# Inverse roots of the norms: a power on GpSimd in place of logarithm, exponential and a Newton step

## The chip, the cores and the metric

The kernel runs on one core of a Trainium2 chip. The metric is the device time of one execution in microseconds (us), lower is better. A core has TensorE (PE, matrix products), VectorE (DVE), ScalarE (ACT), GpSimd (POOL) and SyncE (SP, which only issues transfers here). Each engine runs its own instructions strictly in the order in which they were written; semaphores make it wait for the others.

## The reference, cut to what matters

One step of a one-layer decoder: an RMS norm of x, one wide projection, two attention mixers, gates, and two more projections. Two kinds of norm matter here, that of x over 1024 columns, and that of every q and k head over 64:

```python
def rms_norm(x, gain):
    xf = x.astype(jnp.float32)
    y = xf * lax.rsqrt(jnp.mean(xf * xf, axis=-1, keepdims=True) + NORM_EPS)
    return (y * gain.astype(jnp.float32)).astype(x.dtype)

h = rms_norm(x, norm_gain)
parts = jnp.split(jnp.einsum("ntd,de->nte", h, w_in), SPLIT_POINTS, axis=-1)
a_qkv = [(rms_norm(heads(parts[3 * g]), qk_norm_a[g, 0]),
          rms_norm(heads(parts[3 * g + 1]), qk_norm_a[g, 1]),
          heads(parts[3 * g + 2])) for g in range(A_GROUPS)]
```

There are 1024 prompt positions and 8 decode rows, 1032 columns in all. Everything is float32.

## The kernel before

Activations are held transposed: features on the 128 partitions, the 1032 positions as columns, cut into three chunks (slots) of 344 columns. Float32 products are made of three passes, with each operand split into a rounded part (`hi`, made by an ACT copy) and a rest (`lo`, made by a subtraction on VectorE or POOL).

The projections run over 82 weight tiles of 128 output columns in the order of `ORDER`. Four gate tiles come first, in the start stage, while x is normed. Then follow the tiles of mixer B (g = 3: k, v, q and gates between), then four groups c = 0 to 3 of mixer A, each with q, k and v tiles for g = 0, 1, 2 and two or three gate tiles (`ga`, `gb`), then `zb`, `za`, `br` and `out`. A tile has three slots, a slot 24 dense matmuls (line 248), and a slot three parts of eight matmuls. At each part's end, `part_end` emits attention work and whatever was put there by `after(n, f)`: f is called n parts later. So nothing is planned by costs; the order is what this walk writes.

Per tile the next tile's weights are converted in two halves (`w_conv`, lines 126 and 127: ACT rounds, POOL subtracts), at one and three parts after the tile's first part, and the loading of the tile after that is issued from SP at five parts (there is one staging buffer, which POOL's subtraction releases).

For a q or k chunk, `ev_qk` squares the matmul's result on ACT (line 885), multiplies it with the head's gain on VectorE (line 886) and splits the squares into `sqh` and `sql` (lines 889, 890). Three parts later `ssq` sums the squares over the heads' 64 rows by two matmuls into PSUM (894, 895) and starts the root: Ln, Exp and Square on ACT (225 to 227), and POOL multiplies the gained result by the approximate root (900). Two parts after that `norm` makes Newton's step on VectorE in two operations (230 and 904), the second of which multiplies into the result. There are 87 such chunks: 15 of g = 3 and 72 of mixer A. After the last chunk of a tile, `after_qk` starts the split pieces `prep_q` (ACT 319, POOL 320) and `prep_k` or `prep_k2` (ACT and VectorE, lines 355, 356, 337, 338), which feed the attention's matmuls.

For x itself `h_root` does the same three times in the start stage, once per chunk of columns, with the Newton step written to the root (235); `h_scale` then applies the root (VectorE 215, ACT 216, and POOL or VectorE 221). The roots' tiles are `rn` (two buffers) and `root`; `rt` and `sq` hold the root's square.

Of the kernel before, what the change touches and what calls it, by code (L numbers as in the profile page):

```python
# [10 lines left out]
F32 = mybir.dt.float32  # L11
# [3 lines left out]
ALU = mybir.AluOpType  # L15
# [4 lines left out]
D = 1024  # L20
# [47 lines left out]
def hybrid_step(ctx: ExitStack, tc: tile.TileContext, a):  # L68
# [21 lines left out]
    eps = cst.tile([128, 1], F32, name="eps")  # L90
# [7 lines left out]
    nc.vector.memset(eps, EPS)  # L98
# [86 lines left out]
    def sv(j, k):  # L185
        return sq[min(j, 1)][k]
# [10 lines left out]
    def h_add(j, k):  # L197
        if k > 1:
            nc.vector.tensor_tensor(sv(j, k % 2), sv(j, k % 2), sv(j, k), op=ALU.add)
        if k == KK - 1:  # L200
            nc.vector.tensor_tensor(sv(j, 0), sv(j, 0), sv(j, 1), op=ALU.add)

    def h_root(j):
        pm = psum("w", 4)
        nc.tensor.matmul(pm[:, :CH], ones, sv(j, 0), start=True, stop=True)  # L205
        t = tmp("sq", [128, CH])
        rsqrt_act(roots[j], t, pm[:, :CH], D)
        rsqrt_dve(roots[j], t, pm[:, :CH], D)
# [14 lines left out]
    def rsqrt_act(r, t, ssq, n):  # L223

        nc.scalar.activation(r, ssq, AF.Ln, scale=1.0 / n, bias=eps)  # L225
        nc.scalar.activation(r, r, AF.Exp, scale=-0.5)  # L226
        nc.scalar.activation(t, r, AF.Square)  # L227

    def newton(t, ssq, n):
        nc.vector.scalar_tensor_tensor(ssq, ssq, n * EPS, t, op0=ALU.add, op1=ALU.mult)  # L230

    def rsqrt_dve(r, t, ssq, n):

        newton(t, ssq, n)
        nc.vector.scalar_tensor_tensor(r, ssq, -3.0 * n, r, op0=ALU.add, op1=ALU.mult)
# [642 lines left out]
    def ev_qk(kind, g, c, ch, pt):  # L878
# [11 lines left out]
        after(0, lambda: nc.vector.tensor_tensor(sl, s, sh.bitcast(F32), op=ALU.subtract))  # L890

        def ssq():
# [4 lines left out]
            t = tmp("rt", [128, CH])  # L897
            rsqrt_act(r, t, pm[:, :CH], 64)

            nc.gpsimd.tensor_tensor(dst[:, col], dst[:, col], r, op=ALU.mult)  # L900

            def norm():
                newton(t, pm[:, :CH], 64)
                nc.vector.scalar_tensor_tensor(dst[:, col], pm[:, :CH], -3.0 * 64, dst[:, col], op0=ALU.add, op1=ALU.mult)
                if ch == NCH - 1:
                    after(1, lambda: after_qk(kind, g, c))
# [272 lines left out]
    def conv_consts():  # L1179
        nc.vector.tensor_copy(blk, blk_f)  # L1180
        nc.vector.tensor_scalar(hsel, blk_f[:, ::64], 0.125, None, op0=ALU.mult)
        nc.vector.tensor_scalar(qkg, qkg, -1.0 / 128, None, op0=ALU.mult)
# [55 lines left out]
    nc.vector.tensor_scalar(gain, gain, -0.5 / D, None, op0=ALU.mult)  # L1238
# [181 lines left out]
```

## Time and profile before

| what | value |
|---|---|
| time, median of 2 runs | 1251.02 us (1248.45 to 1253.59) |
| time of the profiled execution | 1251.58 us |
| its span, first to last instruction | 1249.8 us |
| mean granted clock of TensorE | 0.988 of full speed |
| TensorE busy | 1184.3 us, 95% |
| VectorE busy | 786.5 us, 63% |
| ScalarE busy | 785.3 us, 63% |
| GpSimd busy | 631.7 us, 51% |

A row of the profile names the engine, the line of the kernel, the operation, what it writes and reads (out<-in), its shape, how often it ran, its time, and what ended the engine's idle time before it. The time differs from the span by the 1.8 us around the first and last instruction.

### The profile page before, as it was taken

The page shows a single profiled execution, that of the slowest core. Times are in us where ns is not written, and L with a number is a line of the kernel's source. Part 1 is how long each engine was busy: PE and PEld are TensorE (multiplying, and loading weights), DVE is VectorE, ACT ScalarE, POOL GpSimd, SP SyncE. Part 2 cuts the span into 40 slices and gives each one's busy share as a digit, 9 for nine tenths or more (in the row PEclk, how much of TensorE's full clock was granted, in tenths as well). Part 3 has the DMA queues.
Part 4 walks back from the last instruction along what each step waited for, and adds up shares of the span by engine and source line. Part 5 has one row for each costly group of instructions (what it writes and reads, how often), then busy time and mean ns, then how long its engine had stood idle before and what let it go on. Part 6 is the DMA issues. An engine that isn't in the chain of part 4 may idle for free.

```text
span 1249.8 us, 21998 instructions
## 1 busy us (share of the span) xinstructions
PE 1184.3 (95%) x7649; PEld 1150.3 (92%) x7649; DVE 786.5 (63%) x1881; ACT 785.3 (63%) x1879; POOL 631.7 (51%) x613
## 2 busy tenths in 40 slices
PE   7899999999989998989999899998999999999998
PEld 6799999999989997979999798888898898999998
DVE  6853555777757767886779876888756573343111
ACT  5555676787958794868777697857796533443110
POOL 3555244443624564855476673658453585444220
PEclk9999999999999998999999999999899999999999
DMA  6146446366483756556765639464658646543343
GB/s 224 41 144 198 170 152 228 134 207 187 139 249 140 230 171 193 174 168 191 217 190 197 209 137 275 132 216 163 198 153 230 195 158 216 186 144 110 109 147 102
DMA packets 117648, 219.44 MB, mean 176 GB/s; under 512 B 27337, under 2 KB 96801, under 8 KB 116129
## 3 DMA queue, kind: packets, MB, share of 16 engines
q1 hardware_dynamic: 117536, 218.03, 54.5%
q8 instruction: 61, 1.00, 0.3%
q14 instruction: 51, 0.41, 0.1%
HBM read 180.14 MB, written 113.25 MB: 235 GB/s over the span
## 4 chain that ended last, share of the span: by engine, by line
PE 57%; DVE 15%; ACT 13%; DMA 5%; POOL 5%; issue 4%; SPq 1%; POOLq 0%; DVEq 0%; ACTq 0%
PE ps_d L248 43%; PE ps_w L248 4%; ACT P L449 2%; DMA w_st<-in_w 2%; PE ps_w L483 2%; DVE k_b L356 2%; PE ps_o L556 1%; ACT q_st L319 1%; DMA dkv<-in_ca 1%; DVE sql L890 1%; POOL q_st L320 1%; DVE dpr L854 1%; PE ps_w L430 1%; PE ps_w L431 1%; DVE P L439 1%
## 5 line engine op out<-in xcount | busy, mean ns | idle before, releaser
L248 PE MATMUL ps_d<-h_hi,w 128*128 128x344 f32 x3456 | 862.9, 326 | 9.9 <-ACT h_hi L191 6.0
L248 PEld LDWEIGHTS ps_d<-h_hi,w 128*128 128x128 f32 x3456 | 605.7, 191 | 14.8 <-ACT h_hi L191 7.0
L248 PE MATMUL ps_d<-h_lo,w 128*128 128x344 f32 x1728 | 569.8, 330 | 5.9 <-POOL h_lo L221 3.3
L248 PEld LDWEIGHTS ps_d<-h_lo,w 128*128 128x128 f32 x1728 | 329.7, 191 | 10.3 <-POOL h_lo L221 5.8
L127 POOL TENSOR_TENSOR w<-w_st,w 128x512 fp32r<-128x512 f32 (+1 forms) x159 | 212.2, 1337 | 183.7 <-ACT w L126 164.7
L449 ACT ACTIVATE P<-P,st 128x256 f32<-128x256 f32 (+1 forms) x256 | 115.6, 453 | 67.0 <-DVE st L439 51.9
L126 ACT ACTIVATE w<-w_st 128x512 fp32r<-128x512 f32 (+1 forms) x160 | 100.5, 632 | 84.2 <-DMA w_st<-in_w 82.8
L900 POOL TENSOR_TENSOR qn<-qn,rn 128x344 f32<-128x344 f32 x48 | 45.9, 957 | 162.7 <-ACT rn L226 132.4
L320 POOL TENSOR_TENSOR q_st<-qn,q_st 64x512 fp32r<-64x512 f32 x64 | 92.1, 1442 | 24.7 <-ACT q_st L319 18.6
L510 DVE TENSOR_TENSOR pt<-ps_w,pt 128x384 fp32r<-128x384 f32 (+1 forms) x112 | 49.3, 440 | 50.5 <-ACT pt L509 50.0
L509 ACT ACTIVATE pt<-ps_w 128x384 fp32r<-128x384 f32 (+1 forms) x112 | 43.9, 392 | 48.5 <-DVE pt L510 44.1
L483 PE MATMUL ps_w<-ident,P 128*128 128x128 f32 x400 | 63.6, 275 | 3.8 <-DVE sls L770 1.1
L1116 DVE TENSOR_TENSOR xres<-ps_d,xres 128x344 f32<-128x344 f32 x24 | 12.4, 517 | 76.1 <-PE ps_d L248 45.3
L900 POOL TENSOR_TENSOR kn<-kn,rn 128x344 f32<-128x344 f32 x39 | 37.3, 957 | 42.8 <-ACT rn L226 36.3
L890 DVE TENSOR_TENSOR sql<-sq,sqh 128x344 fp32r<-128x344 f32 x87 | 57.9, 666 | 0.6
L483 PEld LDWEIGHTS ps_w<-ident,P 128*128 128x128 f32 x400 | 49.9, 140 | 9.0 <-ACT P L449 2.9
L885 ACT ACTIVATE sq<-ps_d 128x344 f32<-128x344 f32 x87 | 39.3, 452 | 28.7 <-PE ps_d L248 23.3
L319 ACT ACTIVATE q_st<-qn 64x512 fp32r<-64x512 f32 x64 | 54.0, 867 | 0.7
L230 DVE SCALAR_TENSOR_TENSOR ps_w<-ps_w,rt 128x344 f32<-128x344 f32 x87 | 44.9, 516 | 14.7 <-ACT rt L227 14.3
L556 PE MATMUL ps_o<-pt,v 128*128 128x256 f32 (+1 forms) x288 | 46.7, 281 | 6.9 <-DVE pt L510 6.3
L431 PE MATMUL ps_w<-k_b,q_st 128*128 128x128 f32 (+1 forms) x192 | 51.9, 281 | 0.0
L225 ACT ACTIVATE rn<-ps_w,eps 128x344 f32<-128x344 f32 x89 | 47.8, 537 | 6.1 <-PE ps_w L205 4.7
(225 smaller groups left out, 2167.6 us busy)
## 6 DMA issues: line engine op xcount, KB each, us to landing
w_st<-in_w SPq DMA_DIRECT2D x81, 512.0 KB
out_sa<-in_ca SPq DMA_DIRECT2D x16, 1020.0 KB
dkv<-in_ca SPq DMA_DIRECT2D x24, 512.0 KB
sc<-sc_dr SPq DMA_DIRECT2D x32, 192.0 KB
k_b<-k_a SPq DMA_DIRECT2D x18, 256.0 KB
k_a<-k_b SPq DMA_DIRECT2D x18, 256.0 KB
x<-in_xT SPq DMA_DIRECT2D x24, 172.0 KB
oz<-o_dr SPq DMA_DIRECT2D x8, 516.0 KB
```

Of the source, the lines that this page charges most:

```text
L126: nc.scalar.activation(wh, s, AF.Copy)
L127: eng.tensor_tensor(wl, s, wh.bitcast(F32), op=ALU.subtract)
L248: nc.tensor.matmul(pt[:, :CH], ops[i][0], ops[i][1], start=(i == 0), stop=(i == N - 1))
L319: nc.scalar.activation(j.view_o(t[s, :T])[:, c], v, AF.Copy)
L320: nc.gpsimd.tensor_tensor(j.view_o(t[r, :T])[:, c], v, j.view_o(t[s, :T])[:, c].bitcast(F32), op=ALU.subtract)
L431: nc.tensor.matmul(pt[:, o:o + 128 * nk], j.sq[h][:, q], j.sk[h][:, k], start=False, stop=True)
L449: nc.scalar.activation(u.p[:, c], u.p[:, c], AF.Exp, scale=-1.0, bias=st[:, qb, h:h + 1], accum_out=st[:, qb, 2 + h:3 + h])
L483: nc.tensor.transpose(pt[:, o:o + 128], u.p[:, o:o + 128], ident)
L510: nc.vector.tensor_tensor(t[:, 512 + p0:512 + p0 + m], pt[:, o:o + m], t[:, p0:p0 + m].bitcast(F32), op=ALU.subtract)
L556: nc.tensor.matmul(pt[:, c], j.vv[kb // 4][:, v0:v0 + 128], t[:, 512 * n + p0:512 * n + p0 + 128 * nq], start=(first and n == 0), stop=Tru ...
L890: after(0, lambda: nc.vector.tensor_tensor(sl, s, sh.bitcast(F32), op=ALU.subtract))
L900: nc.gpsimd.tensor_tensor(dst[:, col], dst[:, col], r, op=ALU.mult)
```

## The change

The inverse root is no longer made by Ln, Exp, Square and a Newton step. ACT copies the sums out of PSUM, and POOL raises the copy to the power -0.5, with the exponent in a one-column tile `mhalf`, read as if it were 344 columns wide. eps is added where the squares are last touched: in the last addition of `h_add` (as D / 128 * EPS, since 128 rows are summed there) and in the subtraction that makes `sql`. The mean's divisor and Newton's -0.5 go into the gains as constants (32 and 8, the square roots of 1024 and 64). The product with the root moves from `ssq` to `norm`, two parts later, and is made by VectorE for g = 3 and by POOL for the rest. The root's square needs no tile any more.

```diff
         if k == KK - 1:
-            nc.vector.tensor_tensor(sv(j, 0), sv(j, 0), sv(j, 1), op=ALU.add)
+            nc.vector.scalar_tensor_tensor(sv(j, 0), sv(j, 0), D / 128 * EPS, sv(j, 1), op0=ALU.add, op1=ALU.add)
...
         nc.tensor.matmul(pm[:, :CH], ones, sv(j, 0), start=True, stop=True)
-        t = tmp("sq", [128, CH])
-        rsqrt_act(roots[j], t, pm[:, :CH], D)
-        rsqrt_dve(roots[j], t, pm[:, :CH], D)
+        rsqrt(roots[j], pm[:, :CH])
...
-    def rsqrt_act(r, t, ssq, n):
-
-        nc.scalar.activation(r, ssq, AF.Ln, scale=1.0 / n, bias=eps)
-        nc.scalar.activation(r, r, AF.Exp, scale=-0.5)
-        nc.scalar.activation(t, r, AF.Square)
-
-    def newton(t, ssq, n):
-        nc.vector.scalar_tensor_tensor(ssq, ssq, n * EPS, t, op0=ALU.add, op1=ALU.mult)
-
-    def rsqrt_dve(r, t, ssq, n):
-
-        newton(t, ssq, n)
-        nc.vector.scalar_tensor_tensor(r, ssq, -3.0 * n, r, op0=ALU.add, op1=ALU.mult)
+    def rsqrt(r, ssq):
+
+        nc.scalar.activation(r, ssq, AF.Copy)
+        nc.gpsimd.tensor_tensor(r, r, mhalf.to_broadcast([128, CH]), op=ALU.pow)
...
-        after(0, lambda: nc.vector.tensor_tensor(sl, s, sh.bitcast(F32), op=ALU.subtract))
+        after(0, lambda: nc.vector.scalar_tensor_tensor(sl, s, EPS, sh.bitcast(F32), op0=ALU.add, op1=ALU.subtract))
...
             r = tmp("rn", [128, CH], bufs=2)
-            t = tmp("rt", [128, CH])
-            rsqrt_act(r, t, pm[:, :CH], 64)
-
-            nc.gpsimd.tensor_tensor(dst[:, col], dst[:, col], r, op=ALU.mult)
+            rsqrt(r, pm[:, :CH])
 
             def norm():
-                newton(t, pm[:, :CH], 64)
-                nc.vector.scalar_tensor_tensor(dst[:, col], pm[:, :CH], -3.0 * 64, dst[:, col], op0=ALU.add, op1=ALU.mult)
+                (nc.vector if g == 3 else nc.gpsimd).tensor_tensor(dst[:, col], dst[:, col], r, op=ALU.mult)
                 if ch == NCH - 1:
                     after(1, lambda: after_qk(kind, g, c))
...
-        nc.vector.tensor_scalar(qkg, qkg, -1.0 / 128, None, op0=ALU.mult)
+        nc.vector.tensor_scalar(qkg, qkg, 8.0, None, op0=ALU.mult)
...
-    nc.vector.tensor_scalar(gain, gain, -0.5 / D, None, op0=ALU.mult)
+    nc.vector.tensor_scalar(gain, gain, 32.0, None, op0=ALU.mult)
```

The order on POOL in the second group of mixer A (c = 1), from the weights' subtractions ahead of the q tile of g = 1 to the first piece of its split; first before:

```order
L127 TENSOR_TENSOR w<-w_st,w 128x512 x2
L900 TENSOR_TENSOR qn<-qn,rn 128x344 x2
L127 TENSOR_TENSOR w<-w_st,w 128x512
L900 TENSOR_TENSOR qn<-qn,rn 128x344
L127 TENSOR_TENSOR w<-w_st,w 128x512
L900 TENSOR_TENSOR kn<-kn,rn 128x344
L956 COPY dc<-qn 128x8
L320 TENSOR_TENSOR q_st<-qn,q_st 64x512
```

and the same place on POOL with the change, where line 224 is the power and line 889 the product:

```order
L127 TENSOR_TENSOR w<-w_st,w 128x512 x2
L224 TENSOR_TENSOR rn<-rn,mhalf 128x344
L889 TENSOR_TENSOR qn<-qn,rn 128x344
L224 TENSOR_TENSOR rn<-rn,mhalf 128x344
L889 TENSOR_TENSOR qn<-qn,rn 128x344
L127 TENSOR_TENSOR w<-w_st,w 128x512
L224 TENSOR_TENSOR rn<-rn,mhalf 128x344
L127 TENSOR_TENSOR w<-w_st,w 128x512
L889 TENSOR_TENSOR qn<-qn,rn 128x344
L224 TENSOR_TENSOR rn<-rn,mhalf 128x344
L941 COPY dc<-qn 128x8
L309 TENSOR_TENSOR q_st<-qn,q_st 64x512
```

Each chunk has a power of its own on POOL, ahead of the weights' subtractions and of the pieces of the split; the product now stands behind the power, and the one of k's first chunk has moved behind the first piece.

The order on ACT at the same place before, for the first chunk of that q tile:

```order
L885 ACTIVATE sq<-ps_d 128x344
L889 ACTIVATE sqh<-sq 128x344
L225 ACTIVATE rn<-ps_w,eps 128x344
L226 ACTIVATE rn<-rn 128x344
L227 ACTIVATE rt<-rn 128x344
L449 ACTIVATE P,st<-P,st 128x128
```

and on ACT with the change, where line 223 is the copy out of PSUM:

```order
L874 ACTIVATE sq<-ps_d 128x344
L878 ACTIVATE sqh<-sq 128x344
L223 ACTIVATE rn<-ps_w 128x344
L438 ACTIVATE P,st<-P,st 128x128
L438 ACTIVATE P,st<-P,st 128x256
```

Three instructions have become one, and the attention's exponentials (449, now 438) stand directly behind it.

The order on POOL in the start stage with the change, from the weights' last subtraction to the second chunk's first rests (h_lo), where before no row of the root stood on POOL:

```order
L224 TENSOR_TENSOR rn<-rn,mhalf 128x344
L219 TENSOR_TENSOR h_lo<-x_117,h_hi 128x344
L219 TENSOR_TENSOR h_lo<-x_119,h_hi 128x344
L219 TENSOR_TENSOR h_lo<-x_120,h_hi 128x344
L219 TENSOR_TENSOR h_lo<-x_121,h_hi 128x344
L219 TENSOR_TENSOR h_lo<-x_123,h_hi 128x344
L219 TENSOR_TENSOR h_lo<-x_124,h_hi 128x344
L224 TENSOR_TENSOR root<-root,mhalf 128x344
L224 TENSOR_TENSOR rn<-rn,mhalf 128x344
L219 TENSOR_TENSOR h_lo<-x_117,h_hi 128x344
```

The power of the first chunk of columns (`root`) stands directly ahead of that of the third (`rn`), and h_lo behind both.

## Rows read from the trace of the kernel before

**Rows 1.** The page's first part: busy us, share of the span, instructions.

```profile
PE 1184.3 (95%) x7649; PEld 1150.3 (92%) x7649; DVE 786.5 (63%) x1881; ACT 785.3 (63%) x1879; POOL 631.7 (51%) x613
```

**Rows 2.** Two stretches: us, busy us (instructions) of each engine, PEclk, DMA share, GB/s.

```profile
69.00:245.00 176.00, 176.00 (x1187) 173.52 (x1186) 92.74 (x267) 113.81 (x290) 73.84 (x69) 1.00 0.51 174
...
245.00:962.00 717.00, 673.59 (x4420) 651.01 (x4419) 532.79 (x1346) 547.01 (x1353) 397.68 (x398) 0.98 0.60 189
```

**Rows 3.** TensorE's waits, 245 to 962 us: total us, times, longest.

```profile
PE ps_w L791 <- DVE dmx L788: 7.8, 2, 5.1
PE ps_w L895 <- DVE sql L890: 6.4, 5, 2.7
PE ps_o L556 <- DVE pt L510: 6.3, 10, 2.1
```

**Rows 4.** Stretches: the twelve q and k pairs; first, last, sum.

```profile
245.30:278.80 33.50, 33.50 (x235) 33.17 (x234) 24.95 (x67) 27.34 (x71) 16.58 (x15) 1.00 0.63 210
...
869.00:909.40 40.40, 36.78 (x228) 35.01 (x227) 30.46 (x69) 28.73 (x70) 19.98 (x20) 0.92 0.67 233
sum 417.40, PE 394.00 PEld 379.23 DVE 329.89 ACT 310.62 POOL 199.10; mean PE 32.83 PEld 31.60 DVE 27.49 ACT 25.89 POOL 16.59
```

**Rows 5.** Stretches between the pairs: one v tile, two with gate tiles, sum.

```profile
510.60:527.50 16.90, 16.65 (x116) 16.27 (x115) 15.00 (x33) 14.19 (x31) 16.36 (x15) 1.00 0.18 51
...
736.00:771.10 35.10, 32.97 (x213) 31.89 (x212) 22.36 (x61) 28.81 (x74) 20.45 (x23) 0.95 0.55 139
...
909.40:962.30 52.90, 48.08 (x319) 46.89 (x319) 30.45 (x105) 40.24 (x112) 22.39 (x27) 0.97 0.64 177
sum 299.60, PE 279.59 PEld 271.78 DVE 202.86 ACT 236.54 POOL 198.27; mean PE 23.30 PEld 22.65 DVE 16.90 ACT 19.71 POOL 16.52
```

**Rows 6.** Groups by line on POOL: times run, busy us, mean ns, idle before.

```profile
L127 POOL TENSOR_TENSOR w<-w_st,w 128x512 fp32r<-128x512 f32 x155 | 202.4, 1309 | 177.4 <-ACT w L126 158.3 <-DVE sql L890 9.8 <-PE ps_o L556 3.0
...
L900 POOL TENSOR_TENSOR qn<-qn,rn 128x344 f32<-128x344 f32 x48 | 45.9, 957 | 162.7 <-ACT rn L226 132.4
```

**Rows 7.** The same by line on ACT.

```profile
L225 ACT ACTIVATE rn<-ps_w,eps 128x344 f32<-128x344 f32 x89 | 47.8, 537 | 6.1 <-PE ps_w L205 4.7
L226 ACT ACTIVATE rn<-rn 128x344 f32<-128x344 f32 x89 | 43.8, 492 | 2.8
L227 ACT ACTIVATE rt<-rn 128x344 f32<-128x344 f32 x87 | 42.8, 492 | 2.7
...
L1078 ACT ACTIVATE rt<-ps_d 128x344 f32<-128x344 f32 x14 | 6.4, 456 | 5.1 <-PE ps_d L248 3.8 <-issue 1.1
```

**Rows 8.** The same by line on DVE.

```profile
L230 DVE SCALAR_TENSOR_TENSOR ps_w<-ps_w,rt 128x344 f32<-128x344 f32 x87 | 44.9, 516 | 14.7 <-ACT rt L227 14.3
...
L904 DVE SCALAR_TENSOR_TENSOR qn<-ps_w,qn 128x344 f32<-128x344 f32 x48 | 24.8, 517 | 5.7 <-DVE ps_w L230 0.9
```

**Rows 9.** Instructions in time, POOL and then DVE: start us, us.

```profile
569.82 3.16 POOL L320 TENSOR_TENSOR q_st<-qn,q_st 64x512 fp32r<-64x512 f32 x2
...
572.07 1.30 DVE L890 TENSOR_TENSOR sql<-sq,sqh 128x344 fp32r<-128x344 f32 x1
```

**Rows 10.** One line's instructions: duration ns min/median/max, first and last start us.

```profile
L890 DVE TENSOR_TENSOR sql<-sq,sqh x87: 494/518/1956, 74.6 to 912.5; 128x344 fp32r<-128x344 f32 x87
```

**Rows 11.** Instructions in time, start stage: start us, us, [idle before <-releaser].

```profile
23.53 0.55 ACT L225 ACTIVATE rn<-ps_w,eps 128x344 f32<-128x344 f32 x1 [3.56 <-PE ps_w L205]
...
25.71 0.52 DVE L235 SCALAR_TENSOR_TENSOR rn<-ps_w,rn 128x344 f32<-128x344 f32 x1
...
41.45 0.53 ACT L225 ACTIVATE root<-ps_w,eps 128x344 f32<-128x344 f32 x1
...
46.69 0.52 DVE L235 SCALAR_TENSOR_TENSOR rn<-ps_w,rn 128x344 f32<-128x344 f32 x1
...
48.42 2.31 POOL L221 TENSOR_TENSOR h_lo<-x,h_hi 128x344 fp32r<-128x344 f32 x2 [12.32 <-ACT h_hi L216]
...
52.91 0.42 PE L248 MATMUL ps_d<-h_lo,w 128*128 128x344 f32 x1 [0.80 <-POOL h_lo L221]
```

More of the change, by code (lines that the diff above doesn't have):

```diff
@@ L89, in hybrid_step @@
     qkg = cst.tile([128, 8], F32, name="qkg")
-    eps = cst.tile([128, 1], F32, name="eps")
+    mhalf = cst.tile([128, 1], F32, name="mhalf")
     sel = cst.tile([128, 8], F32, name="sel")
@@ L97, in hybrid_step @@
     nsink = cst.tile([128, 8], F32, name="nsink")
-    nc.vector.memset(eps, EPS)
+    nc.vector.memset(mhalf, -0.5)
     nc.vector.memset(dcol, 0.0)
```

## The prediction

> **What bounds the kernel now.** I read the page first, then stretches of time, then the waits, then the single lines that the change touches. The page says that TensorE is busy for 95% of the span, and that GpSimd (POOL) is busy for about half [rows 1]. A share over the whole span hides the stages, so the next view cuts the span. From 69 to 245 us TensorE never stops: 176.0 us busy in 176.0 us. In the attention stage, 245 to 962 us, it is busy 673.6 of 717 us, so 43 us are lost there [rows 2]. The list of what TensorE waited for in that stage is short and scattered, 7.8, 6.4 and 6.3 us at its head, and all three name VectorE (DVE) [rows 3]. So before the change the kernel is TensorE's, and the helpers have room on the average. The room of POOL is the question, because the change gives work to POOL.
>
> A tile here is one weight block of 128 columns, three slots, nine parts. The attention stage has four groups of nine q, k and v tiles and two or three gate tiles. The norms belong to q and k tiles alone, six chunks for each q and k pair, twelve pairs. I cut the stage into these twelve pairs and the twelve stretches between them (v tiles, some with a gate tile behind). The pairs last 417.4 us together, and POOL is busy 199.1 us in them, so 218 us are free [rows 4]. The stretches between last 299.6 us, with POOL busy 198.3: 101 us free, but spread unevenly. Seven stretches are a v tile alone, like the one at 510.6 us, where POOL is busy 16.4 of 16.9 us; those seven have about 10 us free together. The rest is in the five that end with a gate tile [rows 5]. POOL already runs full in every v tile from the second group on, because the v tile inherits merges and decode products.
>
> **The change part by part.** *ScalarE (ACT).* Per chunk Ln, Exp and Square (0.537, 0.492, 0.492 us) go, and a copy of the same shape out of PSUM comes, which the trace has as the gates' copy at 0.456 us [rows 7]. That is 1.07 us less, 90 times: 95 us less ACT work. *VectorE.* Two scalar_tensor_tensor of 0.516 and 0.517 us go, 90 times, 93 us; 15 multiplications for g = 3 come at about the 0.518 us median of a two-input operation of that shape, 8 us [rows 8, 10]. Net 85 us less. Joining eps costs nothing: the same 344 columns are read and written, and the operation is already there.
>
> *GpSimd.* 72 multiplications stay at 0.957 us, 15 leave (14 us), and 90 powers come [rows 6]. The trace has no power. Below nothing is excluded, since it is an added instruction on its engine. The lower bound is the nearest row: the multiplication of the same shape on the same engine with two operands, 0.957 us. From above: ACT works a logarithm and an exponential from tables in one instruction each; POOL's rows are all plain arithmetic, and if it works the power as a series of multiply-add steps, ten such steps at a pass each are 9.6 us. The ends are far apart. The row group it is nearest to is the five instructions whose result it delivers (logarithm, exponential, square, two Newton products): five POOL passes, 5 x 0.957 = 4.8 us. I take 4.8 us and keep 0.96 and 9.6.
>
> [...]
>
> *POOL in the pairs.* 199.1 + 72 x 4.8 = 544.7 us of work in 417.4 us: 127 us too much. What of it can be made up later? A backlog on POOL first hurts the weights: w_conv's two halves stand one and three parts into a tile of nine, and the next tile's matmuls read them about eight parts later, some 14 us in a 16 us tile. Less the 1.3 us of the subtraction itself [rows 6] and its wait, POOL can run some 10 us late before TensorE stands. So each of the five stretches with a gate tile takes back at most about 10 us, and the seven others together 10: 60 us. **+67 us.** Behind a late POOL stand also the q_st pieces, and ACT, which waits in order for the multiplied qn; behind ACT stand the exponentials and the pt copies, for which TensorE's transposes and products wait. That is one delay, not two: POOL goes on with its backlog meanwhile.
>
> *The g = 3 tiles, 69 to 245 us.* 15 powers are 72 us, POOL is free for 176 - 73.8 = 102 us and loses 14 us of products [rows 2]. These powers lie beside TensorE's dense work: **0**. Without this cover, with powers of 9.6 us, 144 against 116 us would add about 28.
>
> *The start.* h_root stands between the squares and the scaled h. From Ln's start to the end of the second Newton product are 26.23 - 23.53 = 2.70 us; copy and power are 0.46 + 4.8 and a hand-over, +2.7. TensorE already waits for h_lo there, so nothing hides it. The roots of columns 0 and 2 follow each other on POOL, which was idle for 12.3 us there. The sums of column chunk 0 are taken up at 41.45, a copy ends at 41.9, its power at 46.7, and the second power at 51.5, against the 47.2 at which the root is done now: +4.3. TensorE waits for that chunk's h_lo too, at 52.91 us [rows 11]. **+7 us.** (The order rows above show both powers directly behind each other.)
>
> *The port.* In the trace a VectorE operation with two SBUF inputs does not start its work while a POOL operation with two SBUF inputs runs: POOL's pair of q_st subtractions ran 569.82 to 572.98, and sql, begun at 572.07, took 1.30 us; the median is 0.518 [rows 9, 10]. [...] In the pairs some 120 such operations (72 sql, 48 k pieces) meet POOL in a power for 346 of 484 us; half a power each is 0.71 x 2.4 x 120 = 204 us. VectorE has 329.9 us now [rows 4], loses 72 x 1.03 = 74, and would have 460 of 484: as full as POOL. Two full in-order engines that wait for each other do not overlap perfectly; I add **+30 us** (bounds 0, if a power lets the port go, and 100, about half the blocked time).
>
> *Relief.* Lighter ACT and VectorE return part of the 43 us only where POOL has room, thus in the gate tiles: **-5 us.**
>
> Sum against the profiled execution's own 1251.6 us (span 1249.8 and 1.8 around it; the median shown is 1251.0, so no correction): 1251.6 + 67 + 0 + 7 + 30 - 5 = **1350 us.**
>
> **The rivals.** *Cheap power, not slower.* If a power costs at most about 3.1 us, the pairs hold 199 + 223 = 422 us, which the gates absorb; the start costs 2 us, the port holds VectorE for about as long as Newton's products did. That gives 1240 to 1270 us. At 0.96 us all of it is hidden, the roots at the start come earlier, and a quarter of the 43 us may return: 1251.6 - 11 = 1240. It decides at a price of about 3.5 us: there 451 us in the pairs is just caught up, with +10 for it, +15 for the port, +3 at the start and -5: 1275, the edge of 2%. For it speaks that POOL's plain operations are all near 1 us; against it that no single POOL row does anything but one arithmetic step. [...] Chance 0.38; within it 0.05 for more than 2% gained, since that wants 25 of the 43 us.
>
> *Long power.* At 6.5 us the pairs hold 667 us: +250 - 60 = +190, start +10, port +30, 1480 us. At eight passes, 7.7 us, 753 us: +276, start +15, g = 3 tiles +8, port +10 (POOL alone is the bound), 1560. At 9.6 us about 1720. For it speaks that the result must be exact enough to need no Newton step any more; against it nothing in the trace. Chance 0.23.
>
> *The port alone.* With a power near 3 us the POOL sum fits, but VectorE could still be stopped in bunches, since the power of one chunk and sql of the next are emitted at the same part's end: +20 to +40, 1270 to 1290. This lies in the forecast's lower edge and is counted there.
>
> **How the numbers follow.** Forecast (3.5 to 6.5 us a power, 1275 to 1480, likeliest 1350): 0.39. Cheap 0.38, long 0.23. About 2% is what a measurement of this kernel tells from no change, 25 us. Faster by more 0.05, within 0.33, slower 0.39 + 0.23 = 0.62. The range from 1240 to 1600 leaves out some 0.07 below and 0.12 above (a power over 8.2 us). The forecast's own range is 1275 to 1480.
>
> **What would show it.** The new POOL line's mean price settles most: under 3.1 the first rival, over 6.5 the second. With 4.8, the pairs' stretches should show POOL at over 95%, their length near 485 to 515 us, TensorE waiting for w and q_st of POOL, sql on VectorE near 2 us in the mean, and the first dense matmuls of columns 1 and 2 some 3 and 7 us later. ACT should lose 95 us of busy time and VectorE's own work 85 us, whatever the time does. I am wrong if POOL is full in the pairs and the pairs are no longer (the catch-up is larger than 60 us), or if the pairs are longer with POOL idle in them (the wait is then elsewhere: the two rn buffers, or the weights' loads on SP's queue that wait for POOL).

## The result and the profile after

| | before | after |
|---|---|---|
| time, median of 2 runs | 1251.02 us (1248.45 to 1253.59) | 6021.8 us (6019.24 to 6024.35) |
| ratio, 95% interval | | 4.809 [4.794, 4.823] |
| span of the profiled execution | 1249.8 us | 6022.6 us |
| mean granted clock of TensorE | 0.988 | 0.604 |

The changed kernel takes almost five times as long. It was predicted slower, at 1350 us with a range from 1240 to 1600; the time is far outside it. The page's first part for the changed kernel (busy us, share of the span, instructions), beside [rows 1]:

```profile
PE 1390.7 (23%) x7649; PEld 1320.1 (22%) x7649; DVE 688.9 (11%) x1716; ACT 692.1 (11%) x1699; POOL 5567.3 (92%) x688
```

POOL went from 631.7 to 5567.3 us, and it is the only engine that is busy for most of the span. ACT lost 93 us and VectorE 98 us. The shares of the chain that ended last say the same, POOL being the first:

```profile
POOL 68%; issue 21%; PE 6%; DVE 2%; ACT 2%; DMA 1%; SPq 0%; POOLq 0%; ACTq 0%; DVEq 0%
```

Two groups of instructions from the page (line, operation, shape, count | busy us, mean ns of one | idle before and what ended it), and for the first, from the view of its line, the duration in ns as min/median/max, with the start of its first and last instruction:

```profile
L224 POOL TENSOR_TENSOR rn<-rn,mhalf 128x344 f32<-128x344 f32 x89 | 4911.4, 55184 | 77.4 <-ACT rn L223 73.9
...
L237 PE MATMUL ps_d<-h_hi,w 128*128 128x344 f32 x3456 | 969.3, 359 | 1594.5 <-POOL w L127 1329.7
```

```profile
L224 POOL TENSOR_TENSOR rn<-rn,mhalf x89: 55145/55157/55612, 25.0 to 5640.5; 128x344 f32<-128x344 f32 x89
```

One power takes 55.2 us. It hardly varies: the shortest and the longest of these 89 differ by 0.5 us, so it is work and no waiting. The other one (the start's `root`) has a row of its own; all 90 are 4966.9 us. The time grew by 4770.8 us. So the new operation itself is as long as the whole loss, and a little longer. The waits below are those of engines that stand behind it, some of the largest sums of the whole run (us in total, times, longest); before, the head of TensorE's list in the attention stage was 7.8 us [rows 3]:

```profile
PE ps_d L237 <- POOL w L127: 1329.7, 26, 57.8
...
ACT k_a L344 <- POOL kn L889: 870.0, 11, 118.6
ACT ot L573 <- POOL n_t L577: 814.2, 16, 59.2
...
ACT rn L223 <- POOL qn L889: 684.6, 16, 52.3
DVE qn L889 <- POOL rn L224: 641.0, 12, 55.1
```

TensorE waits for weights whose subtraction stands behind powers in POOL's queue; ACT waits for multiplied k and q chunks, and for a buffer of the attention's output that an addition of POOL releases. Most of the longest waits are one power long or two.

The same by stage. The columns are the stretch, its us, the busy us (instructions) of PE, PEld, DVE, ACT and POOL, the granted clock, the DMA share and GB/s; the stretches are the start, the g = 3 tiles, the attention stage and the tail:

```profile
0.00:228.90 228.90, 63.80 (x295) 56.66 (x296) 49.82 (x68) 35.06 (x74) 200.72 (x35) 0.63 0.12 40
228.90:1182.30 953.40, 209.16 (x1188) 200.79 (x1188) 96.59 (x244) 95.75 (x254) 885.10 (x66) 0.60 0.09 31
1182.30:5735.50 4553.20, 839.55 (x4419) 786.57 (x4419) 436.69 (x1211) 475.30 (x1217) 4355.56 (x471) 0.58 0.10 30
5735.50:6022.60 287.10, 278.20 (x1753) 276.08 (x1751) 105.78 (x196) 85.96 (x156) 125.94 (x116) 0.99 0.47 154
```

Before, the g = 3 tiles and the attention stage took 176.0 and 717.0 us [rows 2]. Now POOL is busy for 93% and 96% of them and TensorE for 22% and 18%. TensorE's granted clock is 0.60 and 0.58 of full speed there (1.00 and 0.98 before [rows 2]), and 0.99 in the tail, which has no powers and is as long as before. The dense matmuls with `h_hi` took 359 ns in the mean of the whole run, 326 ns before. What the lower clock costs was not measured by itself, but it does not show: in the row of prices below, the time that is left beside the powers is 1060 us at 60 columns, where the mean clock of the run was 0.81, and 1055 us here, where it was 0.60.

### The profile page after: what moved, and what is told of

Same layout as the page of the kernel before. It is cut to its first block, busy times and chain, and to the rows that moved or that the text cites. A ratio compares the mean times of both kernels' runs of the same rounds, so it can differ in the third digit from the quotient of the medians.

```text
span 6022.6 us, 21619 instructions
## 1 busy us (share of the span) xinstructions
PE 1390.7 (23%) x7649; PEld 1320.1 (22%) x7649; DVE 688.9 (11%) x1716; ACT 692.1 (11%) x1699; POOL 5567.3 (92%) x688
## 4 chain that ended last, share of the span: by engine, by line
POOL 68%; issue 21%; PE 6%; DVE 2%; ACT 2%; DMA 1%; SPq 0%; POOLq 0%; ACTq 0%; DVEq 0%
POOL rn L224 63%; PE ps_d L237 5%; POOL w L127 1%; POOL q_st L309 1%; POOL root L224 1%; PE ps_w L237 1%; DMA w_st<-in_w 0%; POOL kn L889 0%; POOL qn L889 0%; DMA dkv<-in_ca 0%; DVE x L213 0%; DVE k_b L345 0%; POOL dkv L761 0%; ACT k_a L344 0%; ACT P L438 0%
## 5 line engine op out<-in xcount | busy, mean ns | idle before, releaser
L224 POOL TENSOR_TENSOR rn<-rn,mhalf 128x344 f32<-128x344 f32 x89 | 4911.4, 55184 | 77.4 <-ACT rn L223 73.9
L237 PE MATMUL ps_d<-h_hi,w 128*128 128x344 f32 x3456 | 969.3, 359 | 1594.5 <-POOL w L127 1329.7
L237 PEld LDWEIGHTS ps_d<-h_hi,w 128*128 128x128 f32 x3456 | 695.6, 219 | 1608.5 <-POOL w L127 1339.0
L237 PE MATMUL ps_d<-h_lo,w 128*128 128x344 f32 x1728 | 626.2, 362 | 4.9 <-DVE h_lo L192 2.6
L237 PEld LDWEIGHTS ps_d<-h_lo,w 128*128 128x128 f32 x1728 | 376.6, 218 | 10.3 <-POOL h_lo L219 5.5
L223 ACT ACTIVATE rn<-ps_w 128x344 f32<-128x344 f32 x89 | 39.9, 449 | 1109.9 <-POOL qn L889 684.6
L419 PE MATMUL ps_w<-k_a,q_st 128*128 128x128 f32 (+1 forms) x192 | 59.2, 325 | 428.4 <-ACT rn L223 324.1
L419 PEld LDWEIGHTS ps_w<-k_a,q_st 128*128 128x128 f32 x192 | 44.0, 229 | 431.2 <-ACT rn L223 326.1
L545 PEld LDWEIGHTS ps_o<-pt,v 128*128 128x128 f32 x288 | 50.0, 220 | 375.2 <-DVE pt L499 373.2
L345 DVE TENSOR_TENSOR k_b<-kn,k_a 64x512 fp32r<-64x512 f32 x36 | 37.1, 1030 | 756.8 <-ACT k_a L344 756.6
```

The lines of the kernel that those rows point to most:

```text
L224: nc.gpsimd.tensor_tensor(r, r, mhalf.to_broadcast([128, CH]), op=ALU.pow)
L237: nc.tensor.matmul(pt[:, :CH], ops[i][0], ops[i][1], start=(i == 0), stop=(i == N - 1))
L419: nc.tensor.matmul(pt[:, o:o + 128 * nk], j.sq[h][:, q], j.ka[h][:, k], start=True, stop=False)
L545: nc.tensor.matmul(pt[:, c], j.vv[kb // 4][:, v0:v0 + 128], t[:, 512 * n + p0:512 * n + p0 + 128 * nq], start=(first and n == 0), stop=Tru ...
```

## The experiments

Three groups of questions: is the price of the power all of it, or does the new order cost something too (first experiment); does the prediction's own sum give the time once the right price stands in it (a row of prices, then the start and the g = 3 tiles alone); and, as it did not quite, why POOL's free time could not be filled. Lengths by stage of all these kernels stand in one table behind the price series.

### The order without the price

POOL multiplies where it would raise to a power, on ACT's copy, which is scaled down (by 1/512, for x by 1/32768); all instructions stand where the changed kernel has them.

```diff
-    def rsqrt(r, ssq):
-        nc.scalar.activation(r, ssq, AF.Copy)
-        nc.gpsimd.tensor_tensor(r, r, mhalf.to_broadcast([128, CH]), op=ALU.pow)
+    def rsqrt(r, ssq, SC=1.0 / 512):
+        nc.scalar.activation(r, ssq, AF.Copy, scale=SC)
+        nc.gpsimd.tensor_tensor(r, r, mhalf.to_broadcast([128, CH]), op=ALU.mult)
```

> The changed kernel with a multiplication in place of the power, so the roots are not computed (the copy is scaled to keep numbers small); all else, order and waits too, is that of the change. Theory A (the price of one power is the whole loss): POOL's operation costs 0.93 to 0.96 us, POOL's sum in the twelve pairs is 199 + 72 x 0.95 = 267 us of 417, everything is hidden, ACT has 95 us and VectorE 85 us less to do: 1240 us, between 1228 and 1252. Theory B (the order costs too: the product two parts later, the power ahead of the weights on POOL, ACT held by the two rn buffers): at least 1300 us, with POOL idle while TensorE waits.

Measured: 1245.81 us against 1249.4 for the kernel before, ratio 0.9975 [0.9965, 0.9985]. Its line 224 in the view of one line (ns min/median/max), and its attention stage (columns as above):

```profile
L224 POOL TENSOR_TENSOR rn<-rn,mhalf x89: 752/762/1208, 24.6 to 913.8; 128x344 f32<-128x344 f32 x89
```

```profile
243.20:952.30 709.10, 670.55 (x4420) 649.88 (x4419) 475.10 (x1201) 475.47 (x1210) 451.96 (x469) 0.98 0.61 191
```

The same instruction in the same place with another arithmetic operation takes 0.76 us in place of 55.2, and the kernel is a quarter of a per cent faster than before. So the new order, the moved product and the hand-overs, taken together with the lighter ACT and VectorE, cost nothing as long as the operation is cheap; 4776 us hang on what POOL does inside this one instruction. It also shows what the change could have given with an operation as cheap as a multiplication: 4 us. That is a sum of gains and losses: in the profiled executions (table below) the start is 2.3 us shorter, the pairs 7 us longer and the stretches between them 15 us shorter.

### A row of prices

The power is done on the first 8, 14, 30 or 60 of the 344 columns only (the others keep the scaled copy), otherwise as in the kernel above. The forecasts for 14, 30 and 60 columns are the prediction's sum with the price that was expected of so many columns (theory A in them: POOL's work alone decides). The forecast for 8 columns is a line between two measured times.

```diff
-        nc.gpsimd.tensor_tensor(r, r, mhalf.to_broadcast([128, CH]), op=ALU.mult)
+        nc.gpsimd.tensor_tensor(r[:, :14], r[:, :14], mhalf.to_broadcast([128, 14]), op=ALU.pow)
```

> The changed kernel with the power on the first 14 of 344 columns alone, so the other roots are not computed. If the price goes by columns (55.2 us for 344, 0.16 us each) one power is 2.3 to 2.5 us. Theory A: POOL's sum in the pairs is 199 + 72 x 2.4 = 372 of 417 us, which is hidden: 1240 to 1262 us. Theory B: above 1300. Theory C (a power holds the port that VectorE's two-input operations need): sql's mean rises above 1 us and the time to about 1275.

> The changed kernel with the power on the first 30 of 344 columns alone, so that one power costs about 4.8 to 5.0 us, the price that the prediction took; the other roots are not computed. Theory A, by the prediction's own sum: pairs 199 + 72 x 4.9 = 552 against 417 us, less 60 caught up, +75, start +7, relief -5, no port term: 1329 us, 1300 to 1350. Theory C (port): another 30, 1350 to 1400, with sql's mean near 2 us.

> The changed kernel with the power on the first 60 of 344 columns alone, about 9.7 us for one power, the upper bound of the prediction; the other roots are not computed. Theory A by the same sum: pairs 199 + 72 x 9.7 = 897 against 417 us, less 60, +420; g = 3 tiles 146 against 116 us, +30; start +22; relief -5: 1719 us, 1680 to 1760. If the loss per us of price is smaller than 72 (POOL not full in the pairs) it comes out well under 1650.

> The changed kernel with the power on the first 8 columns alone, 1.64 us each; the other roots are not computed. Multiplication (0.76 us) gave 1246 us and 14 columns (2.58 us) 1327. Theory D: the loss starts where the product comes later than the ACT instruction that waits for it; on a line between these two it is 1286 us (1270 to 1300). Theory A (hidden until POOL is full): under 1255.

Measured, with the multiplication and the whole power at the ends:

| columns | one operation (us) | time (us) | ratio to before | time less 90 operations (us) |
|---|---|---|---|---|
| multiplication | 0.762 | 1245.81 | 0.9975 [0.9965, 0.9985] | 1177 |
| 8 | 1.64 | 1276.24 | 1.0216 [1.0186, 1.0245] | 1129 |
| 14 | 2.584 | 1327.36 | 1.0624 [1.0598, 1.0649] | 1095 |
| 30 | 5.103 | 1521.76 | 1.218 [1.2152, 1.2207] | 1062 |
| 60 | 9.897 | 1950.26 | 1.561 [1.5573, 1.5646] | 1060 |
| 344 | 55.2 | 6021.8 | 4.809 [4.794, 4.823] | 1055 |

The durations are from the views of the line (8, 14, 30 and 60 columns):

```profile
L224 POOL TENSOR_TENSOR rn<-rn,mhalf x89: 1623/1638/2082, 24.1 to 944.7; 128x8 f32<-128x8 f32 x89
```

```profile
L224 POOL TENSOR_TENSOR rn<-rn,mhalf x89: 2577/2584/3027, 24.3 to 995.7; 128x14 f32<-128x14 f32 x89
```

```profile
L224 POOL TENSOR_TENSOR rn<-rn,mhalf x89: 5090/5103/5554, 25.6 to 1189.2; 128x30 f32<-128x30 f32 x89
```

```profile
L224 POOL TENSOR_TENSOR rn<-rn,mhalf x89: 9883/9897/10342, 23.1 to 1609.6; 128x60 f32<-128x60 f32 x89
```

The sum was too low each time (1240 to 1262, 1300 to 1350 and 1680 to 1760 us forecast for 14, 30 and 60 columns); the line gave 1286 us for 8 columns, and 1276 were measured. The last column is read as follows. From 5 us a power on it stands still: each further microsecond of price costs 90 us, all 90 powers in full, and the kernel is POOL's. Below that the time still hides part of them, but not all even at the cheap end: between 0.76 and 1.64 us the time grows by 30.4 us for 0.88 us of price, 35 powers' worth. The prediction had free room up to 3.1 us and called 3.5 us the point that decides. Measured, the loss is already about 2% at 1.64 us (2.16%, interval 1.86 to 2.45). At the prediction's own price of 4.8 us a straight line between 14 and 30 columns gives an estimated 1498 us, where the sum said 1350.

Where the time lies (us per stage, from stretches cut at the same instructions; g = 3, the twelve q and k pairs together, the stretches between them together, as in [rows 2, 4, 5]):

| kernel | start | g = 3 | pairs | between | tail |
|---|---|---|---|---|---|
| before | 69.1 | 176.2 | 417.3 | 299.7 | 287.5 |
| multiplication | 66.8 | 176.4 | 424.6 | 284.5 | 287.7 |
| 8 columns | 68.1 | 176.2 | 440.6 | 300.6 | 288.8 |
| 14 columns | 72.1 | 176.7 | 462.1 | 328.9 | 287.3 |
| 30 columns | 79.4 | 201.6 | 513.0 | 439.3 | 286.9 |
| 60 columns | 90.7 | 273.7 | 651.8 | 646.4 | 287.7 |
| after | 228.9 | 953.4 | 2143.1 | 2410.1 | 287.1 |

The row of 30 columns is the one nearest to the prediction's price. Its pairs took 513 us, inside the 485 to 515 that the prediction named, but not for its reason: it had POOL busy for over 95% of them, and POOL was busy for 395.8 of the 513.0 us, 77%. Pairs that are longer with POOL idle in them was one of the prediction's own signs of being wrong. The rest stands in the next column: the stretches between grew by 140 us, where the prediction had 60 us of the backlog vanish without a trace.

### The price alone

Fifteen POOL operations behind the last output of the kernel before, each of another shape, value or exponent; nothing reads what they write, so only their durations count.

```diff
+        def pw(n, m, i=0, src=b, op=ALU.pow):
+            nc.gpsimd.tensor_tensor(o[:n, :m], src[:n, :m], ex[:n, i:i + 1].to_broadcast([n, m]), op=op)
+
+        pw(128, 344)
+        pw(128, 172)
...
+        pw(1, 88)
+        pw(128, 90, src=v)
...
+        pw(128, 300, op=ALU.mult)
```

> The kernel before, with 15 operations on POOL behind the last output, so its time is longer by their sum and says nothing else; they price a power by itself. On 128 rows: 344, 172, 86 and 8 columns; then 64 rows x 80, 16 x 82, 8 x 84 and 1 x 88 columns; 90 columns with mixed values instead of 64; exponents 0.5, -1, 2, 1 and 0 on 92 to 100 columns; a multiplication of 300 columns. If the price is one of columns (all rows in step): 55.2, 27.6, 13.8 and 1.4 us, and 80 to 88 columns cost 12.9 to 14.2 us with however few rows. [...] If the price goes by value or exponent, -0.5 differs from 2 and 1. Multiplication: 0.8 us.

Measured, by line with shapes kept apart (count | busy us, ns | idle before); `qb` holds 64 everywhere, `qv` mixed values, `qe` the exponents, which are -0.5 in all of these rows but the one of 96 columns, where it is 2:

```profile
L1120 POOL TENSOR_TENSOR qo<-qb,qe 128x344 f32<-128x344 f32 x1 | 55.4, 55419 | 18.9 <-DVE qe L1115 18.9
...
L1120 POOL TENSOR_TENSOR qo<-qb,qe 128x172 f32<-128x172 f32 x1 | 27.8, 27771 | 0.1
...
L1120 POOL TENSOR_TENSOR qo<-qb,qe 128x96 f32<-128x96 f32 x1 | 15.6, 15616 | 0.1
...
L1120 POOL TENSOR_TENSOR qo<-qv,qe 128x90 f32<-128x90 f32 x1 | 14.7, 14681 | 0.1
...
L1120 POOL TENSOR_TENSOR qo<-qb,qe 1x88 f32<-1x88 f32 x1 | 14.3, 14345 | 0.1
...
L1120 POOL TENSOR_TENSOR qo<-qb,qe 128x86 f32<-128x86 f32 x1 | 14.0, 14042 | 0.1
...
L1120 POOL TENSOR_TENSOR qo<-qb,qe 128x8 f32<-128x8 f32 x1 | 1.6, 1637 | 0.1
...
L1120 POOL TENSOR_TENSOR qo<-qb,qe 128x300 f32<-128x300 f32 x1 | 0.7, 685 | 0.1
```

The price is one of columns: (55419 - 27771) / 172 = 161 ns each, and (55419 - 1637) / 336 = 160. One row costs what 128 cost (14.3 us for 88 columns, between 14.0 for 86 and 14.7 for 90). Mixed values in place of 64 lie on the same line. So do the rows left out here, with 64, 16 and 8 rows (80, 82 and 84 columns in 13.1, 13.4 and 13.7 us) and with the exponents 2, 0.5, -1, 1 and 0, at 15.6, 15.0, 15.3, 16.0 and 16.3 us for 96, 92, 94, 98 and 100 columns: a power of 1 or 2 is not cheaper than one of -0.5. The last row, a multiplication of 300 columns in the same form, is 0.69 us.

### The start alone

The kernel before, with the power for the three roots of x only.

```diff
-        t = tmp("sq", [128, CH])
-        rsqrt_act(roots[j], t, pm[:, :CH], D)
-        rsqrt_dve(roots[j], t, pm[:, :CH], D)
+        rsqrt(roots[j], pm[:, :CH])
```

> The kernel before, with the power for the three roots of x alone; q and k keep logarithm, exponential and Newton. Theory A: the first root is later by 0.46 + 55.2 - 2.7 = 53 us, and of the roots of chunks 0 and 2, which follow each other on POOL, the second ends 2 x 55.2 us after the first copy instead of 5 us, +105: together +158, 1410 us (1390 to 1425). Rival: the two overlap with dense work of the first tiles and cost only about two powers' length, 1360.

Measured: 1412.62 us, ratio 1.131 [1.123, 1.138], +162 us. The three powers in time (start us, us, [idle before <-releaser]), and the wait:

```profile
24.36 55.17 POOL L226 TENSOR_TENSOR rn<-rn,mhalf 128x344 f32<-128x344 f32 x1 [1.26 <-ACT rn L225]
...
95.24 55.21 POOL L226 TENSOR_TENSOR root<-root,mhalf 128x344 f32<-128x344 f32 x1 [5.85 <-ACT root L225]
150.42 55.15 POOL L226 TENSOR_TENSOR rn<-rn,mhalf 128x344 f32<-128x344 f32 x1
```

```profile
PE ps_d L253 <- ACT h_hi L216: 154.5, 3, 103.9
```

The prediction's mechanism holds here: nothing hides the roots at the start, and TensorE waits for two powers in a row (103.9 us is its longest wait).

### The g = 3 tiles alone

The kernel before, with the power for the fifteen chunks of g = 3 only (the rest keeps Ln, Exp, Square and Newton's step).

```diff
-            rsqrt_act(r, t, pm[:, :CH], 64)
-            nc.gpsimd.tensor_tensor(dst[:, col], dst[:, col], r, op=ALU.mult)
+            if g == 3:
+                rsqrt(r, pm[:, :CH])
+            else:
+                t = tmp("rt", [128, CH])
+                rsqrt_act(r, t, pm[:, :CH], 64)
+                nc.gpsimd.tensor_tensor(dst[:, col], dst[:, col], r, op=ALU.mult)
```

> The kernel before, with the power for the 15 chunks of g = 3 alone. Theory A: 15 x 55.2 = 828 us of powers against 102 + 14 us of POOL's free time in that stretch: +712, 1963 us (1900 to 2030), spread over the five q and k tiles and the tiles behind them. Rival: the weights' tolerance of about 10 us per tile makes TensorE wait a whole power each time, and POOL's other work does not fit beside: over 2080 us (15 x 55.2 on top of everything).

Measured: 2026.03 us, ratio 1.622 [1.613, 1.630]. Fifteen powers are 828 us, and the time grew by 776 us: 52 us of them were hidden, where the prediction had a cover of 102 + 14 = 116 us. The two largest kinds of TensorE's waits:

```profile
PE ps_o L563 <- DVE pt L517: 145.8, 11, 49.1
...
PE ps_w L772 <- POOL qx L749: 103.7, 3, 100.6
```

A stage in which TensorE never stopped and POOL was busy for 42% of the time [rows 2] did not give the other 58% away.

### Why POOL's room could not be filled

Everything above leaves one question. In the 30 column kernel POOL has more to do than before but still stands idle for 197 us of the attention stage and 66 us of the g = 3 tiles (first the g = 3 stretch, then the attention stage; columns as above, POOL last of the five):

```profile
79.40:281.00 201.60, 183.31 (x1189) 178.17 (x1188) 95.45 (x251) 97.12 (x259) 135.35 (x67) 0.97 0.45 152
281.00:1233.30 952.30, 750.21 (x4420) 708.57 (x4420) 434.93 (x1203) 474.50 (x1212) 755.42 (x470) 0.87 0.45 142
```

The same idle time remains at 60 columns (1298.2 - 1098.2 = 200 and 67 us) and at 344 (4553.2 - 4355.6 = 198 and 68 us). From 30 columns on it is a fixed sum that no amount of POOL work fills. Below that it falls slowly, in the attention stage from 320 us before over 257 (multiplication), 229 (8 columns) and 212 (14 columns), so the time grows while POOL still idles. One place in the trace of the 30 column kernel shows how that can come about. POOL, then ACT, then VectorE, then TensorE, in time (start us, us, instruction, [idle before <-releaser]):

```profile
644.85 5.11 POOL L224 TENSOR_TENSOR rn<-rn,mhalf 128x30 f32<-128x30 f32 x1
...
653.04 0.91 POOL L889 TENSOR_TENSOR kn<-kn,rn 128x344 f32<-128x344 f32 x1
...
662.94 0.19 POOL L714 COPY dcol<-v_t 128x8 f32<-128x8 f32 x1 [5.20 <-DMA o_dr<-n_t]
...
672.30 1.29 POOL L127 TENSOR_TENSOR w<-w_st,w 128x512 fp32r<-128x512 f32 x1 [2.82 <-ACT w L126]
...
676.04 5.11 POOL L224 TENSOR_TENSOR rn<-rn,mhalf 128x30 f32<-128x30 f32 x1 [2.45 <-ACT rn L223]
```

```profile
653.99 2.15 ACT L344 ACTIVATE k_a<-kn 64x512 fp32r<-64x512 f32 x2 [17.52 <-POOL kn L889]
...
662.43 0.45 ACT L997 ACTIVATE v_t<-ps_d 128x344 f32<-128x344 f32 x1
```

```profile
644.92 0.44 DVE L702 TENSOR_TENSOR n_t<-n_t,sc 128x256 f32<-128x256 f32 x1 [10.58 <-POOL sc L700]
645.29 0.54 DVE L499 TENSOR_TENSOR pt<-ps_w,pt 128x384 fp32r<-128x384 f32 x1
```

```profile
645.89 0.58 PE L545 MATMUL ps_o<-pt,v 128*128 128x256 f32 x1 [6.27 <-DVE pt L499]
...
657.70 1.18 PE L472 MATMUL ps_w<-ident,P 128*128 128x128 f32 x4 [3.62 <-ACT P L438]
```

POOL is late with the power; ACT stands 17.5 us for the product behind it (POOL's row at 653.04). VectorE stands 10.6 us for an addition of POOL (`sc`), and behind that stands its half of the attention weights `pt`, for which TensorE waits 6.3 us. When ACT goes on, TensorE waits another 3.6 us for an exponential (`P`) that comes after the late conversion. When POOL has caught up, it is its turn to wait: 5.2 us for the decode column of v (the view names a transfer, but the copy reads `v_t`, which ACT finished at 662.88), 2.8 us for the rounded weights and 2.5 us for the next sums, all of them work of ACT. So in this place a delay is paid first by ACT, VectorE and TensorE and then by POOL again. Two changes to the 30 column kernel test it. The first starts the split pieces of q and k three parts later, so that ACT's conversion comes to the product when that is done:

```diff
                 if ch == NCH - 1:
-                    after(1, lambda: after_qk(kind, g, c))
+                    after(4 if g < 3 else 1, lambda: after_qk(kind, g, c))
```

> The run with the power on 30 columns (5.1 us each, 1522 us; the other roots are not computed), with the split of a finished q or k tile of mixer A put three parts later. POOL does the same work. Theory D (a loop through ACT: ACT stands in its queue for the product kn or qn that waits behind a power on POOL, behind ACT stand the weights' rounding, the exponentials and pt, and so TensorE and then POOL itself run dry): the 113 + 40 us that ACT stood for kn and qn in the attention stage shrink by about three parts, 5 us, for each of 24 tiles, 60 to 120 us in all: 1400 to 1460 us. Theory A (POOL's work alone): the same time, 1505 to 1540.

Measured: 1496.49 us, ratio 1.198 [1.194, 1.202], 25 us less than 1521.76: more than no effect (1505 to 1540) and far less than the forecast of the loop (1400 to 1460). POOL's idle time in the attention stage fell from 197 to 169 us, about as much as the time. The second gives the roots three buffers in place of two, so that the copy of the sums does not wait for the product two chunks earlier:

```diff
-            r = tmp("rn", [128, CH], bufs=2)
+            r = tmp("rn", [128, CH], bufs=3)
...
-        t = tmp(("sq", "rt", "rn")[ch], [128, CH], bufs=2 if ch == 2 else 1)
+        t = tmp(("sq", "rn", "rn")[ch], [128, CH], bufs=3 if ch else 1)
```

> The run with the power on 30 columns (1522 us; the other roots are not computed), with three buffers for the copied sums instead of two (the gates' copies share them, and the tile rt goes). Theory E (ACT's copy of the sums waits for the product two chunks before it): ACT waited 19 us for this in the attention stage, so 1495 to 1515 us. Theory D: this wait is a by-product, 1510 to 1530.

Measured: 1516.47 us, ratio 1.214 [1.210, 1.218], 5 us less, which two runs of each do not tell from no change (the intervals of the two ratios overlap). As the first of the two could also help the kernel before, it was tried there:

```diff
                 if ch == NCH - 1:
-                    after(1, lambda: after_qk(kind, g, c))
+                    after(4 if g < 3 else 1, lambda: after_qk(kind, g, c))
```

> The kernel before, with the split of a finished q or k tile of mixer A three parts later and nothing else. Control for the same edit beside the power: there the wait it takes away is short (ACT 7 us for VectorE's kn in all), so 1243 to 1255 us, within 0.5% of before; a gain of more than that would be a kernel faster than both.

Measured: 1264.60 us, ratio 1.0117 [1.0093, 1.0142], 1.2% slower, where no more than 0.5% was expected. The late pieces cost 14 us by themselves there. If they cost as much in the 30 column kernel, which no run shows, the wait of ACT's conversion was worth about 40 of its 270 us, and the buffers at most some 5. The waits of the kernel with the late pieces show that the one that was attacked did shrink (119.2 us in the 30 column kernel, k_a for kn), and that TensorE's wait for weights from POOL grew (44.6 us there):

```profile
ACT k_a L344 <- POOL kn L889: 80.2, 11, 13.2
PE ps_d L237 <- POOL w L127: 76.4, 18, 7.1
```

So the loop through ACT's conversion is there, but with the 25 us that were measured it is a small part of the 270. The waits name other things that POOL owes on short notice (q products, weights, the additions of the attention's output and of the merge), but none of them was tested. Which of them hold what share of the 263 us is open, and so is whether they explain all of it.

## Why the prediction was wrong, point by point

**The price of a power: wrong, and nearly all of the miss.** The step took 4.8 us "the five instructions whose result it delivers" with bounds of 0.96 and 9.6 us. Measured are 55.2 us. The upper bound was the step that failed: "ten such steps at a pass each" was a guess at how the operation works, dressed as a bound, and the trace of before had no row that could carry it: every row of POOL there is plain arithmetic, a copy, a fill or a select. For ACT that trace has six table loads (`ACT_TABLE_LOAD`, 1.28 us each), which say nothing of how POOL works. A range for an unknown operation on an engine that has shown only plain ones had no upper end in that trace. The runs give 0.160 us a column and nothing of what happens inside, so it stays open whether the steps were too few or the price of a step too low.

**POOL becomes the bound: right.** The prediction's own sum with 55.2 us in place of 4.8: the pairs 199.1 + 72 x 55.2 - 417.4 - 60 = 3696 us; the g = 3 tiles 15 x 55.2 - 116 = 712; the start 53 + 105 = 158. With 1251.6, and without the terms of the port and the relief, that is 5818 us, 3.4% under the measured 6021.8. The choice of the bound was sound, and with the one term mis-sized by a factor of 11 the answer could not be. The place was not as predicted, though: of the attention stage's 3836 us more, 1726 lie in the pairs and 2110 in the stretches between them.

**"That is one delay, not two: POOL goes on with its backlog meanwhile": wrong, the second miss.** It is worth the 200 us that are left, and at the prediction's price it would have mattered more than the port: the row of prices has an estimated 1498 us at 4.8 us, not 1350. The prediction counted nearly all of POOL's free time as usable: 218 us in the pairs and 60 between them, of 320 us free in the attention stage, and all 102 us in the g = 3 tiles. Measured, POOL's idle time there fell only to 198 and 68 us, however much it had to do; 156 of 422 us were usable. The g = 3 tiles alone hid 52 us of 116. Free time in a row of a stretch is time in which an engine has nothing that it may do yet, and the place shown above has the late engine delay those that feed it; how the whole 200 us divide is open.

**The cheap power's point of decision: wrong by the same step.** With 1.64 us the kernel is 2.2% slower [1.9, 2.5]; the rival had free room up to 3.1 us. Its best case was nearly right: 1240 us forecast, 1245.8 measured with an operation of 0.76 us. In the rival of the long power, the +8 for the g = 3 tiles at 7.7 us does not follow from the prediction's rows: 15 such powers are 115.5 us, inside its cover of 116.

**The start: right.** The roots of columns 0 and 2 follow each other on POOL, nothing hides them, TensorE waits. With the measured price the sum gives +158; the start alone cost +162, and the changed kernel's start stage grew by 159.8 us.

**The port: wrong in its size.** The prediction read from one row that VectorE's operations with two SBUF inputs wait while POOL works on two [rows 9], put half a power of wait on each, and added 30 us (with 0 as its lower bound, if a power lets the port go). In the changed kernel they do wait, but only at a power's start. First a power and the `sql` that begins just after it, POOL and then VectorE:

```profile
671.05 55.16 POOL L224 TENSOR_TENSOR rn<-rn,mhalf 128x344 f32<-128x344 f32 x1 [3.78 <-ACT rn L223]
```

```profile
671.13 1.05 DVE L879 SCALAR_TENSOR_TENSOR sql<-sq,sqh 128x344 fp32r<-128x344 f32 x1
```

Then another power and two that begin later in it:

```profile
2700.34 55.16 POOL L224 TENSOR_TENSOR rn<-rn,mhalf 128x344 f32<-128x344 f32 x1 [4.19 <-ACT rn L223]
```

```profile
2704.99 0.52 DVE L879 SCALAR_TENSOR_TENSOR sql<-sq,sqh 128x344 fp32r<-128x344 f32 x1
...
2710.38 0.52 DVE L879 SCALAR_TENSOR_TENSOR sql<-sq,sqh 128x344 fp32r<-128x344 f32 x1
```

The first took 1.05 us, the other two 0.52 us each, as in [rows 10] where nothing disturbs them. Of the 87, 61 lie wholly inside a power. The 9 that begin in its first 0.31 us took 0.83 to 1.05 us, and all end 1.13 to 1.14 us after the power began; the 52 that begin later took 0.49 to 0.59 us, with a median of 0.507. So the wait ends about 0.62 us into a power of 55.2 us, and the 9 lost some 4 us of VectorE together, where the prediction put 204 us of wait on 120 operations. A median over all 61 (0.508 us) hides this. Beside plain operations the wait lasts nearly to their end: the `sql` of [rows 9] ended 0.39 us after POOL's pair, and in the changed kernel ten products of line 889 that began about 0.06 us into a weights' subtraction of 1.26 us took 1.57 us each, where three with nothing on POOL took 0.52 us. For the power the wait is gone after 0.62 of 55.2 us. That a port is what the two engines wait for, as the prediction calls it, no run shows; the runs show the waits alone, and beside the powers these `sql` waits are some 4 us where the term was 30.

**The relief: right.** ACT lost 93.2 us (95 predicted). VectorE lost 97.6 us (85 predicted of its own work; what more it lost isn't split up here). The worth of it, 5 us, was not measured by itself; the kernel with the multiplication, which has this relief and the new order together, gained 4 us.

**What the changed profile should show.** The line's mean price was named as what settles most, and it did. The pairs are full of POOL (2026.8 of 2143.1 us, 94.6%), TensorE waits for `w`. `sql` near 2 us in the mean, which was to show the port, isn't there.

## What to carry to other kernels

Before a new operation is moved to an engine, its price has to come from a row of that operation on that engine; where there is none, an upper bound made of likely steps is none, and one small experiment (the operation on a few columns, and on twice as many) settles it. Swapping the operation for a cheap one in the same place splits a change into its order and its price in one run. An engine's free time in a stage isn't room for more work when other engines wait for it in order and then feed it: here 156 of 422 us could be filled, and the loss began between 0.76 and 1.64 us a power.

## What the runs showed of the hardware that was not expected

POOL's power of float32 costs 0.16 us per column of the tile, 55.2 us for 344 columns, 72 times the multiplication of the same form in the same place (0.762 us). The price per column was the same for 1 to 128 rows, for the values and for the six exponents tried (13.1 to 16.3 us for 80 to 100 columns). Of the 128 x 344 roots of a chunk only 2 x 344 differ (one for each head and position), and 688 values on 128 rows are 6 columns: from the 128x8 and 128x344 rows an estimated 1.3 us. By the row of prices that lies between the multiplication (0.25% faster) and 8 columns (2.2% slower), before the price of moving the values; it was not run.

Of the VectorE operations with two SBUF inputs that were read beside a power, only those that began at its start were held up. With 344 columns the wait ended 0.62 us into the 55.2 us, seen on `sql` (9 of them, 0.83 to 1.05 us) and on two products of line 889 (1.07 us in place of 0.52); the 52 `sql` that began later ran at a median of 0.507 us.

The multiplication with a one-column operand read as 344 columns wide took 0.762 us in the median, the one with two full operands 0.930 us in the kernel before (its mean in [rows 6], 0.957 us, has some longer ones in it). Here the form with one narrow operand took 18% less.
